# Turning softmax weights on TensorE: 128 queries at a time, or pairs of 64 on the two halves of the array's rows

## The chip, the cores and the metric

The kernel runs on one core of one Trainium2 chip. The metric is device time in microseconds. The other seven cores are idle.

## What is computed

The reference is a two-layer trunk over 256 latent tokens with 256 context tokens as a prefix, model width 1024. Each layer has a token-mixing part (a convolution branch, attention with 8 heads of 64, and gates) and a gated MLP with a short convolution. All is fp32. The part that the change touches is the attention:

```python
s_win = jnp.einsum("bhqd,bhiqjd->bhqij", q_r, k_win, preferred_element_type=jnp.float32) * scale
...
s_ctx = jnp.einsum("bhqd,bhcd->bhqc", q_r, k_ctx, preferred_element_type=jnp.float32) * scale
s = jnp.concatenate([s_win.reshape(b, h, GRID_W, n_win), s_ctx], axis=-1)
p = jax.nn.softmax(s, axis=-1).astype(v.dtype)
...
return (jnp.einsum("bhqij,bhiqjd->bhqd", p_win, v_win)
        + jnp.einsum("bhqc,bhcd->bhqd", p_ctx, v_ctx))
```

Latent queries see a window of latent keys (a bias that masks all other latent keys stands in for the window here) and all 256 context keys, so 512 keys in all. Context queries see the 256 context keys; they are computed in the first layer alone.

## The kernel before

Activations lie with channels on the partitions and tokens along the free dimension. A weight comes as a unit of 128 x 1024 in fp32 by a load on SP's queue (L155), is split into a high and a low part, `whi` by ScalarE (L158) and `wlo` by VectorE (L159), and each product is then three matmuls (L177, L178, L179). The buffers `raw`, `whi` and `wlo` rotate through four places each, so a load is issued only when the split of an earlier unit has freed its place. Loads of other weights (`in_wada`, L145) use the same places of `raw`, and the load of `sb` (`across`, L243, with a Silu in L245) stands behind them in SP's queue.

Side work is threaded between the matmul groups: each group calls `slot()`, which advances a list of generators by one step. Two of these matter here. `conv_run` and `layer_norm` put the 31 taps of the depthwise convolution on VectorE (L576, one instruction for a tap), and `Attention.step` does a step of the attention. The framework then orders the instructions of each engine ahead of time by its own estimates of their durations; `issue_after` adds constraints to that order. On the chip each engine takes its instructions in that order.

The attention goes by pairs of heads j (0 to 3); a pair's two heads lie on partitions 0 to 63 and 64 to 127. A step does three things in this order:

- `turn`: the softmax weights of the last step are turned, so that keys come onto the partitions.
- `values`: the weights that were turned in the step before are multiplied with V (L502), and the result is split into `oh` and `ol` (L508, L509).
- `products`: the scores of the next work item (L430). Two heads go at a time, on rows 0 to 63 and 64 to 127 of the array, into two banks. The softmax follows on VectorE (L448: bias and maximum; L453) and on ScalarE (L451: exponential; L454: scaling). For context queries these are L462, L467, L469 and L472.

A work item has four score tiles `pp` of 128 queries x 512: for latent queries two blocks of 128 queries by two heads; for context queries two heads by two pairs, each with two blocks of 128 queries by 256 keys side by side. Layer 0 has four latent items and two of context queries, layer 1 four latent ones, so `turn` runs ten times.

In `turn` each 128 x 128 block of `pp` is transposed by TensorE (L484, L489), with the block as the stationary operand and the identity as the moving one. Four blocks of one head fill one PSUM bank, and ScalarE copies the bank to `pT` (L485, L490). The banks are two of tag `sc`, then one of tag `pt` and one of the four of tag `main`; `products` then uses the same four tags. `values` reads `pT` as the moving operand, 256 queries wide.

Of the kernel before, what the change touches and what calls it, by code (L numbers as in the profile page):

```python
# [8 lines left out]
F32 = mybir.dt.float32  # L9
# [6 lines left out]
P = 128  # L16
# [3 lines left out]
S = 256  # L20
# [12 lines left out]
LAT, CTX = slice(0, S), slice(S, 2 * S)  # L33
# [12 lines left out]
def trunk(ctx: ExitStack, tc: tile.TileContext, xt, cvec, crow, wall, wada, params, bias_t, rope_t, out):  # L46
    nc = tc.nc
    pe, act, dve, pool, sp = nc.tensor, nc.scalar, nc.vector, nc.gpsimd, nc.sync
# [11 lines left out]
    def nm(s):  # L60
        uid[0] += 1
        return f"{s}_{uid[0]}"
# [3 lines left out]
    def psum(tag="main"):  # L66
        return psp.tile([P, 512], F32, tag=tag, bufs=BANKS[tag], name=nm(tag))

    def tmp(w=512):
        return tp.tile([P, w], F32, tag="t", bufs=5, name=nm("t"))  # L70
# [4 lines left out]
    def sl(w, i):  # L75
        return w[:, i * P : (i + 1) * P]
# [29 lines left out]
    start = ExitStack()  # L106
# [5 lines left out]
    ident = cp.tile([P, P], F32, name="ident")  # L112
# [260 lines left out]
    HALF = [slice(0, HD), slice(HD, P)]  # L373

    class Attention:
# [99 lines left out]

        def turn(self, what, its, pps):

            pts = [self.eb.tile([P, 4, S], F32, tag="pT", bufs=4, name=nm("pT")) for _ in range(2)]
            for n, tags in enumerate((("sc", "sc"), ("pt", "main"))):
                for i, pp in enumerate(pps[n]):  # L480
                    pt = psum(tags[i])
                    if what == LAT:
                        for kt in range(4):
                            pe.transpose(sl(pt, kt), sl(pp, kt), ident)  # L484
                        act.copy(pts[i][:, :, n * P : (n + 1) * P], pt.rearrange("p (k q) -> p k q", k=4))  # L485
                    else:
                        for t in range(2):
                            for kt in range(2):
                                pe.transpose(pt[:, kt * S + t * P : kt * S + (t + 1) * P], sl(pp, 2 * t + kt), ident)  # L489
                        act.copy(pts[i][:, 2 * n : 2 * n + 2, :], pt.rearrange("p (k q) -> p k q", k=2))  # L490
            js = [its[0][0]] if what == LAT else [it[0] for it in its]
            self.pv.append((what, js, pts))

        def values(self, what, js, pts, bank):
            po = psum(bank)
            kts = range(4) if what == LAT else range(2, 4)
            for n, j in enumerate(js):
                c = slice(n * S, (n + 1) * S)
                for kt in kts:
                    for i in range(2):  # L500
                        h = 2 * j + i
                        pe.matmul(  # L502
                            po[i * HD : (i + 1) * HD, c], self.V[kt][:, h * HD : (h + 1) * HD],
                            pts[i][:, 2 * n + kt - kts[0], :], start=kt == kts[0], stop=kt == kts[-1],
                        )
            for n, j in enumerate(js):
                c = slice(n * S, (n + 1) * S)
                act.copy(self.oh[j][:, what], po[:, c])  # L508
                dve.tensor_tensor(self.ol[j][:, what], po[:, c], self.oh[j][:, what].bitcast(F32), ALU.subtract)  # L509
# [11 lines left out]
    for k in range(KD):  # L521
        sp.dma_start(x[k], xt[k])
        q = tmp()
# [19 lines left out]
    for l in range(DEPTH):  # L543
# [5 lines left out]
        with ExitStack() if last else start as e1a:  # L549
# [68 lines left out]
            with ExitStack() as e1b:  # L618
# [98 lines left out]
                else:  # L717
                    sp.dma_start(rope, rope_t)
                    pg0 = [psum("sc") for _ in range(2)]
                    for uu in range(2):  # L720
                        wg = wunit(l, U_GLU0 + uu)
                        for i in range(2):
                            for kk in range(4):
                                k = 4 * uu + kk
# [59 lines left out]
                n = 0  # L784
# [16 lines left out]
            with ExitStack() as e1c:  # L801
# [71 lines left out]
                for n, pc in branch(U_CO, sh_, sl_):  # L873
                    t = tmp()[:, :T]
# [60 lines left out]
        with ExitStack() as e2:  # L935
# [115 lines left out]
            for streams, ns in [((0, 1), range(NB)), *(((s,), range(NB, KD)) for s in range(NS))]:  # L1051
                wu = None
                c = slice(streams[0] * S, (streams[-1] + 1) * S)
                for n in ns:
                    ps = psum()
                    for k in range(KF):
                        t = n * KF + k
# [19 lines left out]
            if last:  # L1077
                std, rs = small([P, 2], "red"), small([P, 2], "rs")
                pt = psum("pt")
# [133 lines left out]
```

## Time and profile before

| | |
|---|---|
| Median of 3 runs | 1129.97 us (1129.38 to 1132.16) |
| Span of the profiled execution, first to last instruction | 1127.4 us; what lies around it is not told apart, and the median is 2.6 us above the span |
| Granted TensorE clock | 0.998 |
| TensorE matmuls / weight loads, busy | 1115.5 us (99%) / 965.1 us (86%) |
| VectorE busy | 906.5 us (80%) |
| ScalarE busy | 565.7 us (50%) |
| Transposes in `turn` | 160: 128 in L484, 32 in L489 |
| Copies to `pT` | 40: 32 in L485, 8 in L490 |
| Conv taps L576 | 240, 140.6 us busy |

Times in views of the profile are microseconds from the start of the span. PE is TensorE's matmuls, PEld its weight loads, DVE is VectorE, ACT is ScalarE, SPq is SP's queue. Lines such as L484 are lines of the kernel. A view of the timeline gives start, duration, engine, line, operation, what is written from what, the shape (rows x columns of the stationary operand, then partitions x elements), and how many instructions are merged into the row; a bracket shows idle time and what ended it. The chain of waits gives start, duration and what the end of the program waited for at that time. The view of waits gives who waited for whom, microseconds in total, times, longest.

### The profile page before, as it was taken

What the parts mean: (1) busy time and instruction counts of PE and PEld (TensorE: products, weight loads), DVE (VectorE), ACT (ScalarE), POOL (GpSimd) and SP (SyncE); (2) the same over time, 40 slices, a digit from 0 to 9 for tenths busy, and PEclk for the clock granted to TensorE, in tenths of its full rate; (3) what the DMA queues carried; (4) which work ended last, traced back from release to release, by engine and by line L of the source; (5) the groups of instructions that cost most, each with busy time, mean ns of one, the idle gap of its engine ahead of it and who ended that gap; (6) DMA issues with size and microseconds to landing.
All of it is one profiled execution on the core that took longest, in us unless ns stands there. A gap on an engine that the chain in (4) does not pass through costs nothing.

```text
span 1127.4 us, 17780 instructions
## 1 busy us (share of the span) xinstructions
PE 1115.5 (99%) x6854; PEld 965.1 (86%) x6854; DVE 906.5 (80%) x1625; ACT 565.7 (50%) x937; POOL 17.2 (2%) x24
## 2 busy tenths in 40 slices
PE   9999999999999999999999999999999999999997
PEld 7678777787789988888888888989898999999997
DVE  4689999786778788888898555789996898988773
ACT  4347657542334543444334223544677667766642
POOL 0000000000000000000000000010000000000000
PEclk9999999999999999999999999999999999999999
DMA  8832231635734354545556656555533575665781
GB/s 325 310 100 89 92 117 38 200 99 198 248 120 145 110 170 133 184 152 155 165 181 205 214 188 197 176 194 174 154 109 120 180 247 175 187 193 182 213 274 57
DMA packets 53941, 190.83 MB, mean 169 GB/s; under 512 B 6240, under 2 KB 6496, under 8 KB 53856
## 3 DMA queue, kind: packets, MB, share of 16 engines
q1 hardware_dynamic: 53568, 189.65, 52.6%
q8 instruction: 54, 0.88, 0.3%
q14 instruction: 31, 0.25, 0.1%
q10 hardware_dynamic: 288, 0.04, 0.0%
HBM read 188.62 MB, written 1.05 MB: 168 GB/s over the span
## 4 chain that ended last, share of the span: by engine, by line
PE 85%; DVE 10%; DMA 2%; ACT 2%; issue 1%; POOL 0%; SPq 0%; DVEq 0%; ACTq 0%; POOLq 0%
PE main L177 25%; PE main L179 24%; PE main L178 24%; DVE cb L576 4%; PE main L629 4%; DVE wlo L159 2%; DMA raw<-in_wall 1%; PE sc L127 1%; PE sc L177 1%; PE sc L179 1%; PE sc L178 1%; PE po L200 1%; PE po L502 1%; DMA sb<-in_crow 1%; PE sc L430 0%
## 5 line engine op out<-in xcount | busy, mean ns | idle before, releaser
L177 PE MATMUL main<-h,whi 128*128 128x256 f32 (+1 forms) x1328 | 446.8, 337 | 0.0
L179 PE MATMUL main<-h,wlo 128*128 128x256 f32 (+1 forms) x1328 | 443.4, 335 | 0.5 <-DVE wlo L159 0.5
L178 PE MATMUL main<-h,whi 128*128 128x256 f32 (+1 forms) x1328 | 442.4, 333 | 0.0
L158 ACT CAST whi<-raw 128x1024 fp32r<-128x1024 f32 (+1 forms) x244 | 252.5, 1039 | 284.7 <-PE main L178 128.6
L159 DVE TENSOR_TENSOR wlo<-raw,whi 128x1024 fp32r<-128x1024 f32 (+1 forms) x244 | 293.7, 1209 | 113.3 <-ACT whi L158 108.6
L177 PEld LDWEIGHTS main<-h,whi 128*128 128x128 f32 x1328 | 249.5, 188 | 32.0 <-issue 3.9
L179 PEld LDWEIGHTS main<-h,wlo 128*128 128x128 f32 x1328 | 249.5, 188 | 28.9 <-DVE wlo L159 0.7
L178 PEld LDWEIGHTS main<-h,whi 128*128 128x128 f32 x1328 | 249.9, 188 | 28.1 <-issue 0.2
L576 DVE SCALAR_TENSOR_TENSOR cb<-u,par,cb 128x512 f32<-128x512 f32 (+1 forms) x240 | 140.6, 620 | 1.2
L261 DVE CUSTOM_DVE_ANT_0 t<-raw,sb,par 128x1024 bf16<-128x1024 f32 x100 | 126.9, 1280 | 1.4 <-ACT sb L245 1.2
L177 PE MATMUL main<-fh,whi 128*128 128x256 f32 (+1 forms) x386 | 123.0, 319 | 0.0
L178 PE MATMUL main<-fl,whi 128*128 128x256 f32 (+1 forms) x386 | 122.9, 319 | 0.0
L179 PE MATMUL main<-fh,wlo 128*128 128x256 f32 (+1 forms) x386 | 122.9, 318 | 0.0
L178 PEld LDWEIGHTS main<-fl,whi 128*128 128x128 f32 x386 | 72.7, 188 | 5.6
L177 PEld LDWEIGHTS main<-fh,whi 128*128 128x128 f32 x386 | 72.7, 188 | 5.6
L179 PEld LDWEIGHTS main<-fh,wlo 128*128 128x128 f32 x386 | 72.7, 188 | 5.5
L948 ACT ACTIVATE t<-main,par 128x512 f32<-128x512 f32 (+1 forms) x82 | 50.7, 669 | 35.3 <-PE main L179 35.3
L949 DVE SCALAR_TENSOR_TENSOR t<-main,par,t 128x510 f32<-128x510 f32 (+1 forms) x82 | 47.6, 616 | 8.2 <-ACT t L948 7.6
L952 DVE SCALAR_TENSOR_TENSOR t<-main,par,t 128x510 f32<-128x510 f32 (+1 forms) x82 | 46.6, 611 | 0.0
L356 ACT ACTIVATE h<-t,mod 128x256 fp32r<-128x256 f32 x56 | 25.2, 502 | 37.5 <-DVE t L355 37.4
L883 DVE SCALAR_TENSOR_TENSOR x<-main,mod,x 128x256 f32<-128x256 f32 x48 | 22.1, 480 | 23.6 <-PE main L179 23.4
L629 PE MATMUL main<-whi,h 128*128 128x512 f32 x128 | 40.6, 402 | 0.0
(217 smaller groups left out, 1198.0 us busy)
## 6 DMA issues: line engine op xcount, KB each, us to landing
raw<-in_wall SPq DMA_DIRECT2D x239, 512.0 KB, 4.2
raw<-in_wada SPq DMA_DIRECT2D x88, 512.0 KB, 4.4
bias<-in_bias_t SPq DMA_DIRECT2D x8, 640.0 KB, 4.4
row<-in_wada SPq DMA_DIRECT2D x8, 512.0 KB, 4.8
sb<-in_crow SPq DMA_DIRECT2D x5, 512.0 KB, 6.1
x<-in_xt SPq DMA_DIRECT2D x8, 256.0 KB, 4.6
raw<-in_wall SPq DMA_DIRECT2D x8, 256.0 KB, 6.8
out<-t SPq DMA_DIRECT2D x3, 256.0 KB, 2.1
```

What stands on the lines that cost most here:

```text
L158: act.copy(hi[:, c], r[:, c])
L159: dve.tensor_tensor(lo[:, c], r[:, c], hi[:, c].bitcast(F32), ALU.subtract)
L177: pe.matmul(ps, w[0], xh, start=start, stop=False)
L178: pe.matmul(ps, w[0], xl, start=False, stop=False)
L179: pe.matmul(ps, w[1], xh, start=False, stop=stop)
L261: dve.tensor_tensor_reduce(tmp().bitcast(BF16), r, v, 1.0, pr(l, BADA + n, 1), ALU.mult, ALU.add, mods[l][:, n, s : s + 1])
L356: high = act.activation(hi[:, c], y[:, c], AF.Identity, bias=b)
L576: dve.scalar_tensor_tensor(cb[j], src, w, cb[j], ALU.mult, ALU.add)
L629: pe.matmul(pv[t], h1[n == 1][k][:, c], w[n == 2][:, b], start=k + n == 0, stop=k == KD - 1 and n == 2)
L948: act.activation(c, pv_, AF.Identity, bias=pr(l, FDB + t, 1), scale=w[1])
L949: dve.scalar_tensor_tensor(c[:, :, 1:], pv_[:, :, : S - 1], w[0], c[:, :, 1:], ALU.mult, ALU.add)
L952: dve.scalar_tensor_tensor(c[:, :, : S - 1], pv_[:, :, 1:], w[2], c[:, :, : S - 1], ALU.mult, ALU.add)
```

## The change

A block of 128 queries is transposed as two matmuls of 64 queries, one on rows 0 to 63 of the array and one on rows 64 to 127. The first writes 64 columns of one bank and the second 64 columns of another. So the two banks of a pair of score tiles fill together: a bank now holds one half of the queries of both tiles, where it held all queries of one. ScalarE copies a bank with runs of 64 elements where it had 128, as many elements and as many copies as before. `pT` is one tile for both heads in place of two, with the same bytes and the same layout for `values`, which is otherwise unchanged. For context queries the four blocks of a tile are taken in the order that puts them into the same places as before. In the changed file, lines after `turn` have a number one higher.

```diff
         def turn(self, what, its, pps):
 
-            pts = [self.eb.tile([P, 4, S], F32, tag="pT", bufs=4, name=nm("pT")) for _ in range(2)]
+            pT = self.eb.tile([P, 2, 4, S], F32, tag="pT", bufs=2, name=nm("pT"))
             for n, tags in enumerate((("sc", "sc"), ("pt", "main"))):
+                outs = [psum(t).rearrange("p (i s q) -> p i s q", i=2, s=4) for t in tags]
                 for i, pp in enumerate(pps[n]):
-                    pt = psum(tags[i])
+                    for s in range(4):
+                        src = s if what == LAT else s % 2 * 2 + s // 2
+                        for pt, r in zip(outs, HALF):
+                            pe.transpose(pt[:, i, s], sl(pp, src)[r], ident[r, r])
+                for pt, r in zip(outs, HALF):
                     if what == LAT:
-                        for kt in range(4):
-                            pe.transpose(sl(pt, kt), sl(pp, kt), ident)
-                        act.copy(pts[i][:, :, n * P : (n + 1) * P], pt.rearrange("p (k q) -> p k q", k=4))
+                        act.copy(pT[:, :, :, n * P + r.start : n * P + r.stop], pt)
                     else:
-                        for t in range(2):
-                            for kt in range(2):
-                                pe.transpose(pt[:, kt * S + t * P : kt * S + (t + 1) * P], sl(pp, 2 * t + kt), ident)
-                        act.copy(pts[i][:, 2 * n : 2 * n + 2, :], pt.rearrange("p (k q) -> p k q", k=2))
+                        to = pT[:, :, 2 * n : 2 * n + 2].rearrange("p i k (t q) -> p i (k t) q", t=2)
+                        act.copy(to[:, :, :, r], pt)
             js = [its[0][0]] if what == LAT else [it[0] for it in its]
-            self.pv.append((what, js, pts))
+            self.pv.append((what, js, pT))
 
-        def values(self, what, js, pts, bank):
+        def values(self, what, js, pT, bank):
...
                         pe.matmul(
                             po[i * HD : (i + 1) * HD, c], self.V[kt][:, h * HD : (h + 1) * HD],
-                            pts[i][:, 2 * n + kt - kts[0], :], start=kt == kts[0], stop=kt == kts[-1],
+                            pT[:, i, 2 * n + kt - kts[0]], start=kt == kts[0], stop=kt == kts[-1],
                         )
```

## The prediction

> **What bounds the kernel now.** I read the page first, for the busy shares and the chain that ended last.
>
> ```profile
> PE   1115.5 (99%) x6854; PEld 965.1 (86%) x6854; DVE 906.5 (80%) x1625; ACT 565.7 (50%) x937; POOL 17.2 (2%) x24
> ...
> PE 85%; DVE 10%; DMA 2%; ACT 2%; issue 1%; POOL 0%; SPq 0%; DVEq 0%; ACTq 0%; POOLq 0%
> ```
>
> TensorE is busy nearly always, but a tenth of the chain is VectorE's. So the question is which engine ends last in the two stretches with attention (about 84 to 205 us, and 800 to 872). Busy time by stretch comes next: span, then PE, PEld, DVE, ACT.
>
> ```profile
> 160.00:180.00 20.00, 20.00 (x114) 15.80 (x113) 20.00 (x40) 13.95 (x26) 0.00 (x0) 1.00 0.33 102
> ...
> 820.00:840.00 20.00, 20.00 (x147) 17.35 (x146) 19.91 (x58) 15.29 (x34) 0.04 (x1) 1.00 0.41 129
> ```
>
> Both engines are full there, and the conv taps (L576) are what fills VectorE. What decides is the place where one of the two has to wait. The chain of waits, in order of time, shows it for layer 0:
>
> ```profile
> core 0 of [0], span 1127.4 us
> ...
> 198.98 0.75 DVE cb L576
> ...
> 200.73 1.15 DVE wlo L159
> ...
> 202.27 6.08 DMA sb<-in_crow
> ...
> 212.03 0.44 PE pt L224 x2
> ```
>
> VectorE's queue reaches a weight split (L159), which frees a buffer; only then does SP's queue issue the load of sb, ScalarE puts that through Silu, evicts the modulation products behind it in its queue, and TensorE may do the transposes of L224. TensorE gets there first. The view of waits:
>
> ```profile
> PE pt L224 <- ACT t L217: 1.1, 1, 1.1
> ```
>
> So up to 212.0 us layer 0 ends by VectorE's queue, and TensorE has 1.1 us to spare.
>
> **The transposes themselves.** Ten turns (eight for latents, two for context), each with 16 transposes. One turn in the chain, and the instructions of the line (min/median/max ns):
>
> ```profile
> 827.98 0.87 PE sc L484 x8
> 828.85 0.44 PE pt L484 x4
> 829.29 0.44 PE main L484 x4
> 829.73 1.88 PE po L502 x16
> ```
>
> ```profile
> L484 PEld LDWEIGHTS sc<-ident,pp x64: 138/141/144, 102.5 to 859.1; 128*128 128x128 f32 x64
> L484 PE MATMUL sc<-ident,pp x64: 270/272/275, 102.7 to 859.2; 128*128 128x128 f32 x64
> ```
>
> A turn takes 0.87 + 0.44 + 0.44 = 1.75 us, 109 ns for each transpose. The change makes it 32 transposes of 64 rows with 64 moving columns, alternating between the halves of the rows. The built program shows just that: 320 of 128x64 in place of 160 of 128x128, and nothing else moved on TensorE. Two things can set the new step. By the moving columns, half of 109 is 55 ns. By the weight load it depends on how long a transposing load holds the loader, because each half still loads 128 columns of pp. The nearest rows are plain loads:
>
> ```profile
> 12.80 1.86 PEld L517 LDWEIGHTS pt<-one,t 128*128 128x128 f32 x16 [0.41 <-issue]
> ```
>
> ```profile
> L502 PEld LDWEIGHTS po<-pT,V x144: 132/137/137, 113.8 to 869.4; 128*64 128x64 f32 x144
> ```
>
> L517 moves one column, so its pace is the loader's: sixteen loads in 1.86 us, less the length of one (0.19, as in the loads of L430 below), over 15, is 111 ns for 128 plain columns. The transposing load, at 141 ns, lasts as long as the plain load of 64 columns, 137; its hold is then about half of 111, some 57 ns. Bounds: 55 and 111 ns for a load; I take 57, by L502. Whether the halves work at once is shown by the products of 64 rows:
>
> ```profile
> 116.65 0.28 PE L430 MATMUL pt<-qk,qk 64*128 64x256 f32 x1
> 116.76 0.28 PE L430 MATMUL main<-qk,qk 64*128 64x256 f32 x1
> 116.77 0.28 PE L430 MATMUL pt<-qk,qk 64*128 64x256 f32 x1
> 116.88 0.28 PE L430 MATMUL main<-qk,qk 64*128 64x256 f32 x1
> ```
>
> ```profile
> 116.53 0.19 PEld L430 LDWEIGHTS sc<-qk,qk 64*128 64x128 f32 x1
> 116.53 0.19 PEld L430 LDWEIGHTS pt<-qk,qk 64*128 64x128 f32 x1
> ```
>
> Each half goes on every 120 ns, so two matmuls pass in 120, and two loads start at the same time. Hence 16 pairs x 57 = 0.91 us in place of 1.75.
>
> The Trainium skill (TensorE: Matmul & The Clock Gate, LDWEIGHTS (loading the stationary operand)) speaks against the change: a load's time goes with its columns, and 32 rows take as long as 128. L517 and L502 agree for plain loads (111 ns of pace for 128 columns). For transposing loads no row shows the pace; if it held there too, the pair would take what one transpose takes now.
>
> Going between whole-array and half-array work costs something as well:
>
> ```profile
> 829.66 1.49 PEld L502 LDWEIGHTS po<-pT,V 128*64 128x64 f32 x16 [0.17 <-issue]
> 831.53 0.53 PEld L430 LDWEIGHTS sc<-qk,qk 64*128 64x128 f32 x6 [0.39 <-issue]
> ```
>
> Some 0.2 us for one switch (0.39 holds the pace of an L502 pair, 0.2). The skill says the same (TensorEngine Tiling (Array Packing), Key Properties: a change of tiling mode drains the array). The change adds one switch ahead of the transposes. In the first turn of a layer, where products follow directly, one goes away again.
>
> Net on TensorE: 0.91 + 0.2 - 1.75 = -0.64 us for a turn that values follow.
>
> In the first turn of each layer that is worth nothing, because the products that follow wait for ScalarE's four copies, one after another:
>
> ```profile
> 105.04 0.61 ACT L485 COPY pT<-main 128x512 f32<-128x512 f32 x1
> ```
>
> ```profile
> 105.53 0.39 PE L430 MATMUL main<-qk,qk 64*128 64x512 f32 x1
> ```
>
> A copy of sc must now wait for both banks, 8 pairs (0.46 us) and the switch in place of 4 transposes (0.44): the copies start 0.2 us later there. The copies move as many elements in runs of 64 instead of 128; I cost that at nothing, and at most 0.1 us each.
>
> **What the saved time is worth.** Eight turns (five in layer 0, three in layer 1) x 0.64 = 5.1 us is the most. In layer 0 (four latent and two context turns) TensorE only arrives earlier at L224, where it waits for VectorE's queue: worth 0. Moreover the scheduler has put VectorE's instructions in another order. Of those that stand ahead of the split at 200.73 there is one more in the changed program, a conv tap: 0.75 us by the row at 198.98, somewhat less where its successor doesn't depend on it. VectorE has no idle time to take it up. Taken: +0.7.
>
> In layer 1 TensorE runs without a wait, but VectorE and ScalarE are close behind. The last softmax, and what it leads to:
>
> ```profile
> 852.29 0.48 DVE L576 SCALAR_TENSOR_TENSOR cb<-u,par,cb 128x256 f32<-128x256 f32 x1
> 852.69 0.69 DVE L448 CUSTOM_DVE_ANT_1 sc<-sc,bias 128x512 f32<-128x512 f32 x1
> ```
>
> ```profile
> 867.05 2.99 ACT L158 CAST whi<-raw 128x1024 fp32r<-128x1024 f32 x3
> ```
>
> ```profile
> 868.18 3.50 DVE L159 TENSOR_TENSOR wlo<-raw,whi 128x1024 fp32r<-128x1024 f32 x3 [0.52 <-ACT whi L158]
> ```
>
> ```profile
> 870.29 0.28 PE L179 MATMUL main<-h,wlo 128*128 128x256 f32 x1
> ```
>
> L448 waits for nothing but its turn behind the taps. ScalarE then runs exponentials, scalings, sigmoids and copies back to back up to the casts at 867.05; the first of the three splits ends about 868.18 + 1.2 = 869.4, and TensorE wants it at 870.29. That leaves 0.9 us. In the changed program two more taps stand ahead of that L448, 2 x 0.4 to 0.5 = about 1.0 us. So the split comes 0.1 us after TensorE's old time, and whatever TensorE saved in three turns (1.9 us) is lost in this wait. Bounds: if ScalarE has slack that I don't see, the 0.9 + 1.0 turns into a gain of up to 1.2; if the taps cost 0.6 each, the loss is 0.3. Taken: +0.2.
>
> Sum: +0.7 + 0.2 = +0.9 us on a span of 1127.4. The median of the runs, 1129.97, lies 2.6 above that span, and I carry that over: 1130.9. A difference under 0.3% (3.4 us) is about what a measurement of this kernel can't tell from none.
>
> **The rivals.**
>
> *The weight load sets the pace* (the page's rule above, taken for transposing loads): 16 pairs x 111 = 1.78, with the switch 1.98, +0.23 a turn. In layer 0, 6 x 0.23 = 1.4 stays under the room at L224 (1.1 + 0.7); in layer 1 the first copies start 0.6 later and three turns add 0.7, about 1.3 in place of my 0.2. Total +2.0: 1132.0; with 120 ns a pair, as L430 goes, +3. For: each half loads 128 columns. Against: the 141 ns.
>
> *The halves don't run at once and every transpose keeps its 109 ns*, because it isn't its columns that set it: 32 x 109 + 0.2 = 3.69, +1.94 a turn. Ten turns 19.4, less the 1.1 of room at L224: +18, 1148. It decides from 116 ns a pair on (1.8 us of room in six turns of layer 0); halfway, at 170 ns, six turns cost 6.9 - 1.1 and four 4.6, so +10. For: no row has two transposes at once, and 64 instructions in 0.91 us are denser than any stretch of the trace. Against: L430's rows.
>
> *VectorE doesn't hold and TensorE's time gets through*: -5.1, 1124.9. The load of sb would have to be issued that much earlier; the full VectorE speaks against it.
>
> **How the numbers follow.** My case 0.57, alone 1129.3 to 1132.3; load-bound 0.20, a quarter of it over 0.3%; one at a time 0.15, between 1134 and 1148; getting through 0.08. Within 0.3%: 0.57 + 0.15 = 0.72. Slower: 0.15 + 0.05 = 0.20. Faster: 0.08. The range takes in the first two cases and the mild half of the third: 1128.7 to 1137.
>
> **What would show it.** Right: transposes of a half 55 to 60 ns apart and two at once, a turn of about 0.9 us; the wait at L224 grown from 1.1 to some 5 us (five turns x 0.64, and the later tap); the load of sb issued 0.7 us later in its stage; TensorE waiting for a split near 870 us. Wrong: pairs 110 ns or more apart (second case), single transposes 109 apart (third), L224 without a wait or earlier than 212 us (fourth), or a total more than 3 us off.

## The result, and the profile after

The changed kernel takes 1135.25 us in the median of its first 5 runs (1131.49 to 1139.76), against 1129.97 for the kernel before: a ratio of 1.0042, 95% interval 1.0024 to 1.0061. In a later comparison, beside 23 runs of the kernel before, it was 1135.64 against 1131.89, ratio 1.0049 (1.0030 to 1.0068). So it is slower: both intervals lie above 1. The ratios are above 0.3%, which the prediction took for the least that can be told from none, but the intervals reach down to 0.24 and 0.30%. The profiled execution has a span of 1133.5 us, 6.1 more than before.

The page of the changed kernel, busy shares and shares of the chain:

```profile
PE 1117.4 (99%) x7014; PEld 962.3 (85%) x7014; DVE 906.8 (80%) x1625; ACT 564.6 (50%) x937; POOL 17.2 (2%) x24
...
PE 81%; DVE 12%; ACT 3%; issue 2%; DMA 1%; POOL 0%; DVEq 0%; ACTq 0%; SPq 0%; POOLq 0%
```

The totals hardly tell anything: 160 more matmuls, 1.9 us more of TensorE. The transposes themselves did what was meant. The end of a turn in layer 1, in the timeline of the changed kernel:

```profile
849.87 0.71 PE L485 MATMUL sc<-ident,pp 64*128 64x64 f32 x16
850.42 0.22 PE L485 MATMUL pt<-ident,pp 64*128 64x64 f32 x1
850.42 0.22 PE L485 MATMUL main<-ident,pp 64*128 64x64 f32 x1
850.48 0.22 PE L485 MATMUL pt<-ident,pp 64*128 64x64 f32 x1
850.48 0.22 PE L485 MATMUL main<-ident,pp 64*128 64x64 f32 x1
...
851.01 0.65 PE L503 MATMUL po<-pT,V 128*64 128x256 f32 x4
```

Two halves start at the same time, and pairs follow every 60 to 63 ns. From the first transpose to the first of the values it is 1.14 us.

To see where the time goes I compare the start of one and the same gate or weight product (L177 to L179; same number in TensorE's order) in two traces. The table gives, for each kernel that ran, how much later than in the first profile of the kernel before it starts, in us, at seven places named by that profile's time. 22.6 us lies ahead of every instruction that any of these kernels moves, 184.4 behind the latent turns of layer 0, 212.5 behind L224, 737.8 at the end of layer 0, 870.2 at the end of attention in layer 1, 925 ahead of a normalization in layer 1, and 1118 at the end. Where the text says, as the prediction does, that layer 0 ends early or late, it means the end of its attention, at 212.5 us.

| Kernel | 22.6 | 184.4 | 212.5 | 737.8 | 870.2 | 925 | 1118 |
|---|---|---|---|---|---|---|---|
| changed, first profile | 3.07 | 1.80 | 3.96 | 4.66 | 5.34 | 5.37 | 6.01 |
| changed again (e1) | -0.55 | -1.79 | 0.29 | 1.20 | 1.87 | 1.96 | 4.78 |
| latents alone (e2) | -0.49 | -1.14 | -1.45 | -1.46 | -0.86 | -0.81 | -0.19 |
| context alone (e3) | 0.63 | 0.03 | 0.21 | 0.25 | 0.19 | 0.25 | 3.45 |
| held taps (e4) | 0.62 | -0.50 | 5.04 | 5.94 | 6.89 | 6.84 | 9.97 |
| before, L217 first (e5) | -0.14 | -0.20 | -1.54 | -1.88 | -1.91 | -1.93 | -1.51 |
| changed, L217 first (e6) | 0.00 | -1.26 | 0.69 | 1.09 | 1.78 | 1.74 | 5.74 |
| and values first (e7) | 3.27 | 2.02 | 3.38 | 3.86 | 5.06 | 5.12 | 6.42 |
| and softmax first (e8) | 0.04 | -1.19 | 1.67 | 2.27 | 0.49 | 0.49 | 5.00 |
| changed, square first (e9) | 3.29 | 2.02 | 4.39 | 4.86 | 5.47 | 5.43 | 6.53 |
| before, square first (e10) | 0.36 | 0.33 | 0.07 | -0.28 | -0.25 | -0.27 | 0.65 |
| halves, eased (e11) | -0.17 | -0.75 | -1.05 | -1.01 | -2.78 | -2.78 | -1.56 |
| whole, eased (e12) | 0.01 | -0.01 | -1.35 | -1.37 | -1.43 | -1.44 | -0.77 |

Half of the 6.01 us of the first profile were there before the change could act. Stretches of the changed kernel's start (span, then busy time and count of PE, PEld, DVE, ACT, POOL, then granted clock, DMA share, GB/s):

```profile
12.00:16.00 4.00, 4.00 (x37) 3.17 (x36) 0.16 (x1) 0.00 (x0) 0.12 (x1) 0.77 1.04 419
16.00:20.00 4.00, 4.00 (x24) 3.47 (x17) 1.37 (x5) 1.30 (x3) 0.90 (x1) 0.50 1.03 396
```

The granted clock was 0.50 for 6.8 us there, where the profile of before has 1.00:

```profile
16.00:20.00 4.00, 4.00 (x26) 3.21 (x25) 3.36 (x9) 2.80 (x7) 0.06 (x1) 1.00 1.01 394
```

A second half clock stands in the last context turn of layer 0, as TensorE's timeline and two stretches show:

```profile
194.39 0.71 PE L485 MATMUL sc<-ident,pp 64*128 64x64 f32 x16
196.25 0.27 PE L485 MATMUL pt<-ident,pp 64*128 64x64 f32 x1 [1.14 <-ACT pp L472]
...
196.64 0.27 PE L485 MATMUL pt<-ident,pp 64*128 64x64 f32 x1
...
197.04 0.27 PE L485 MATMUL pt<-ident,pp 64*128 64x64 f32 x1
...
197.76 1.28 PE L503 MATMUL po<-pT,V 128*64 128x256 f32 x8
```

```profile
195.10:198.50 3.40, 2.02 (x25) 1.32 (x26) 3.33 (x7) 3.38 (x10) 0.00 (x0) 1.00 0.00 0
198.50:201.90 3.40, 3.40 (x15) 1.92 (x12) 3.22 (x6) 3.39 (x7) 0.00 (x0) 0.50 0.00 0
```

TensorE comes early, and then waits for one scaling (L472) after another. The stretch with 2.02 us of work in 3.40 is followed by one at half the clock. The same turn in the kernel before has no wait:

```profile
193.40:196.80 3.40, 3.40 (x29) 2.33 (x28) 3.22 (x6) 3.37 (x7) 0.00 (x0) 1.00 0.02 5
```

In layer 1 the values of the last item now wait. Timeline rows of the changed kernel:

```profile
858.45 0.69 DVE L448 CUSTOM_DVE_ANT_1 sc<-sc,bias 128x512 f32<-128x512 f32 x1
...
872.51 0.39 ACT L509 CAST oh<-po 128x256 fp32r<-128x256 f32 x1
872.93 0.42 DVE L510 TENSOR_TENSOR ol<-po,oh 128x256 fp32r<-128x256 f32 x1 [6.01 <-ACT oh L509]
873.41 1.30 PE L503 MATMUL po<-pT,V 128*64 128x256 f32 x10 [0.69 <-DVE ol L510]
```

In the kernel before they follow without a wait, 0.42 us behind the end of `ol`:

```profile
867.23 0.42 DVE L509 TENSOR_TENSOR ol<-po,oh 128x256 fp32r<-128x256 f32 x1 [6.01 <-ACT oh L508]
...
868.07 1.95 PE L502 MATMUL po<-pT,V 128*64 128x256 f32 x16
```

So the first reading was: a start that has nothing to do with the change (if it is chance), two places that the change made late, and a clock that reacts to the waits. The experiments take these apart.

### The profile page after: what moved, and what is told of

Its sections match the earlier page's. It is cut to its first block, busy times and chain, and to the rows that moved or that the text cites. A ratio compares the mean times of both kernels' runs of the same rounds, so it can differ in the third digit from the quotient of the medians.

```text
span 1133.5 us, 18094 instructions
## 1 busy us (share of the span) xinstructions
PE 1117.4 (99%) x7014; PEld 962.3 (85%) x7014; DVE 906.8 (80%) x1625; ACT 564.6 (50%) x937; POOL 17.2 (2%) x24
## 3 DMA queue, kind: packets, MB, share of 16 engines
HBM read 188.62 MB, written 1.05 MB: 167 GB/s over the span
## 4 chain that ended last, share of the span: by engine, by line
PE 81%; DVE 12%; ACT 3%; issue 2%; DMA 1%; POOL 0%; DVEq 0%; ACTq 0%; SPq 0%; POOLq 0%
PE main L177 23%; PE main L179 23%; PE main L178 23%; DVE cb L577 5%; PE main L630 4%; DVE wlo L159 3%; DMA raw<-in_wall 1%; PE sc L127 1%; PE sc L177 1%; PE sc L179 1%; PE sc L178 1%; PE po L200 1%; ACT whi L158 1%; ACT pp L467 1%; ACT pp L472 1%
## 5 line engine op out<-in xcount | busy, mean ns | idle before, releaser
L177 PE MATMUL main<-h,whi 128*128 128x256 f32 (+1 forms) x1328 | 447.2, 337 | 0.0
L179 PE MATMUL main<-h,wlo 128*128 128x256 f32 (+1 forms) x1328 | 443.5, 335 | 0.4 <-DVE wlo L159 0.4
L177 PEld LDWEIGHTS main<-h,whi 128*128 128x128 f32 x1328 | 249.6, 188 | 32.4 <-issue 4.7
L179 PEld LDWEIGHTS main<-h,wlo 128*128 128x128 f32 x1328 | 249.7, 188 | 29.0 <-DVE wlo L159 0.7
L177 PE MATMUL main<-fh,whi 128*128 128x256 f32 (+1 forms) x386 | 123.0, 319 | 0.0
L179 PE MATMUL main<-fh,wlo 128*128 128x256 f32 (+1 forms) x386 | 122.9, 318 | 0.0
L177 PEld LDWEIGHTS main<-fh,whi 128*128 128x128 f32 x386 | 72.7, 188 | 5.6
L179 PEld LDWEIGHTS main<-fh,wlo 128*128 128x128 f32 x386 | 72.7, 188 | 5.6
```

Of the source, the lines that this page charges most:

```text
L177: pe.matmul(ps, w[0], xh, start=start, stop=False)
L179: pe.matmul(ps, w[1], xh, start=False, stop=stop)
```

## The experiments

**e1: the changed kernel again.** No edit.

> The changed kernel once more, unedited. Its first profile lost 3.1 us before 22 us, where TensorE's granted clock was 0.50 for 6.8 us, ahead of every instruction that the change touches; from there to the end it lost another 3.0. Theory A (the early half clock falls at random, the loss behind it belongs to the change): runs fall into two groups, near 1132.2 (1133.5 - 3.1 + 1.8) without the early half clock and near 1135.3 with it; a profile without it starts layer 0 level with the kernel before and ends 2 to 3 us behind. Rival B (the early half clock belongs to the changed program): every run at 1135 or more, and every profile with 0.50 ahead of 22 us.

Median 1135.64 us (1134.22 to 1141.59); the profile has 1.00 throughout the start and starts 0.55 us ahead. So rival B falls: the early half clock doesn't come with the change each time, and it comes without it too. In the 14 profiles of this study it comes in six (6.8 us long in three, 3.4 in three), e3 among them, and e10, which is the kernel before but for an order near 934 us. But the long form was seen in three of the seven profiles with halves in all turns and in none of the seven others. Nothing that the change moves lies ahead of it, yet so few profiles don't exclude that it is more frequent there. A stretch of e10:

```profile
16.00:20.00 4.00, 4.00 (x21) 3.75 (x20) 3.55 (x7) 2.94 (x6) 0.00 (x0) 0.70 1.02 397
```

But theory A was wrong in its times: without the early half clock this execution still took 1134.22 us, since something came that the first profile had not. In the context turn TensorE lost 1.6 us without a half clock (the stretch with 2.15 us of work stayed at 1.00), and L224 ended layer 0 by the load of sb. Stretch, waits, and chain of e1:

```profile
190.00:193.40 3.40, 2.15 (x28) 1.36 (x26) 3.32 (x7) 3.40 (x13) 0.00 (x0) 1.00 0.00 0
```

```profile
PE pt L224 <- ACT t L217: 1.6, 1, 1.6
```

```profile
201.47 1.15 DVE wlo L159
...
203.01 5.63 DMA sb<-in_crow
...
210.00 2.00 ACT sb L245 x2
...
212.32 0.44 PE pt L224 x2
```

From the start to 212.5 us e1 loses 0.84, as the first profile lost 0.89 with a half clock and no wait at L224: two causes of like size, of which the later one counts. Then, behind 925 us, where nothing was changed, e1 loses 2.8:

```profile
PE pt L326 <- DVE ss L312: 1.8, 1, 1.8
```

```profile
928.49 4.70 DMA raw<-in_wall
...
934.25 0.41 ACT t L308
```

```profile
934.10:937.50 3.40, 1.58 (x14) 1.38 (x13) 2.81 (x6) 3.16 (x7) 0.00 (x0) 1.00 0.79 288
937.50:940.90 3.40, 3.40 (x18) 3.40 (x18) 2.49 (x4) 1.98 (x3) 0.70 (x1) 0.51 0.96 306
```

A cast that waits for a weight load stands in ScalarE's queue ahead of a square on whose sum TensorE waits (0.5 us in the profile before, by the row below); and a half clock follows the wait.

```profile
PE pt L326 <- DVE ss L312: 0.5, 1, 0.5
```

**e2: halves in the latent turns alone.**

```diff
+                if what == LAT:
...
+                else:
+                    for i, (pp, t) in enumerate(zip(pps[n], tags)):
+                        pt = psum(t)
...
+                            for t in range(2):
+                                for kt in range(2):
+                                    pe.transpose(pt[:, kt * S + t * P : kt * S + (t + 1) * P], sl(pp, 2 * t + kt), ident)
```

> Halves for the eight latent turns alone; the two context turns are transposed by 128 queries as before. VectorE's order is that of the changed kernel, later taps and all. Theory A (in layer 0 the changed kernel loses in its last context turn: TensorE waits 1.1 us for scalings, and a half clock follows there): no wait and no half clock in that turn, L224 waits again for the load of sb that comes 0.7 us late; layer 0 ends 0.7 to 0.9 behind, layer 1 adds 1.4 by its later softmax: span 1129.7, time 1131.5, plus 3.1 if the early half clock falls. Rival C (the context softmax is late by VectorE's order, whatever the turn): TensorE waits in the context turn here too, the half clock comes all the same, and the time is that of the changed kernel, 1132.2.

Median 1132.23 us beside 1131.89 (ratio 1.0008, 0.9994 to 1.0023). No half clock, as theory A says; but the context softmax is 1.3 us late here too, by VectorE's order, and TensorE loses 1.0 us in that turn, so rival C is half right. And layer 0 ended 0.96 early, not 0.7 late. ScalarE's timeline shows why:

```profile
205.09 0.37 ACT L217 COPY t<-sc 128x256 f32<-128x256 f32 x1
208.70 1.28 ACT L245 ACT_TABLE_LOAD   x1 [3.24 <-DMA sb<-in_crow]
209.99 2.01 ACT L245 ACTIVATE sb<-sb 128x1024 f32<-128x1024 f32 x2
```

The framework happened to put L217 ahead of the Silus, so the load of sb (as late as in e1) stops nobody. Layer 1 loses 0.60 as the changed kernel does.

**e3: halves in the context turns alone.** The condition of e2 is turned round (`what == CTX`); VectorE's softmaxes then have as many taps ahead of them as in the kernel before.

> Halves for the two context turns alone; latent turns as before. VectorE's order is exactly that of the kernel before. Theory A: with the softmax in its old place TensorE reaches the last context turn no earlier than before, so it waits at most 0.3 us there, no half clock; two turns save 1.2 us, which ends in the wait at L224; layer 1 is as before: span 1127.4, time 1129.2 to 1130.0. Rival D (transposes by halves make the half clock by themselves, being short and sparse): the clock falls to 0.5 near 198 us, and L224 comes 1 to 2 us late: 1130.5 to 1132.

Median 1132.80 us (ratio 1.0017, 1.0002 to 1.0033). No wait and no half clock in the context turns: rival D falls, transposes by halves don't bring the half clock by being short. Layer 0 ends 0.42 ahead of its start, layer 1 loses nothing. The 3.2 us at the end are the wait at 934 us with its half clock.

**e4: the taps held back.**

```diff
             def conv_tap(j, t):
+                m = min(AT[tap_at.n], len(tap_at.mx))
+                tap_at.n += 1
+                if m:
+                    with tc.issue_after(tap_at.mx[m - 1].ins):
+                        return conv_do(j, t)
+                return conv_do(j, t)
```

`AT` holds, for each tap, how many softmax instructions of VectorE stood ahead of it in the kernel before.

> The changed kernel with each conv tap kept behind the softmax behind which it stood before (an ordering constraint alone; no work added), so every L448 and L462 has as many taps ahead of it as in the kernel before, and the split ahead of the load of sb has one less than before. Theory A (the later taps are what the change costs): no wait in the context turns beyond 0.5 us, no half clock there, sb at its old time or 0.4 us earlier, and in layer 1 the three turns save up to 1.9 us of which 0.9 to 1.9 gets through: span 1126 to 1127.4, time 1128 to 1129.5. Rival E (the halves cost by something other than VectorE's order): at least 2 us behind the kernel before, as the changed kernel is without its early half clock.

Median 1140.36 us (ratio 1.0084, 1.0067 to 1.0102), the slowest of all: theory A's repair fails. In layer 1 the last L448 has the old number of taps ahead of it and is still 1.3 us late against 737.8. The reason is in the distance from a tap to its successor. Set beside the order of the built program, every tap whose successor is a tap of the same buffer `cb` takes some 0.12 us longer: 0.52 us in place of 0.40 in layer 1, 0.79 in place of 0.66 in layer 0. Ahead of the first L462 of the last context item the kernel before has 5 such pairs and e4 22; in layer 1, ahead of the last L448, 11 and 18. By that estimate they cost 2.0 and 0.8 us. That L462, which has its old 97 taps ahead of it, is 1.9 us late. In layer 0 TensorE waits 4.0 us for scalings, and the clock halves for two stretches:

```profile
PE pt L491 <- ACT pp L478: 4.0, 2, 2.9
```

```profile
192.90:196.30 3.40, 0.67 (x8) 0.40 (x8) 3.33 (x7) 3.38 (x10) 0.00 (x0) 1.00 0.53 154
196.30:199.70 3.40, 2.03 (x14) 1.35 (x16) 3.22 (x6) 3.39 (x8) 0.00 (x0) 0.50 0.00 0
```

**e5: the kernel before with L217 ahead of the Silus.**

```diff
-        with tc.issue_after(lastev[0].ins):
-            act.activation(t, t, AF.Silu)
...
-                        yield from ada_all([(0, 8)])
+                        ev = ada_rows(ada_products(0, 8, "sc"))
+                        silu_of(sb0)
+                        yield
+                        yield
+                        ada_sums(0, 8, ev)
```

> The kernel before, with ScalarE's copy of the modulation products (L217) put ahead of the two Silus that wait for the load of sb; nothing else moved. Theory F (layer 0 of the kernel before ends by VectorE's queue through the load of sb, and by nothing else): the wait of 1.1 us at L224 goes, the next groups follow 1.1 us earlier than in the kernel before at the same start, and the median falls by about 1.1 us. Rival G (another wait stands right behind it): less than 0.3 us.

Median 1128.92 us beside 1131.18 (ratio 0.9984, 0.9973 to 0.9994): faster than the kernel before. Layer 0 ends 1.34 us earlier, counted from 184.4: theory F.

**e6: the same order in the changed kernel.** The edit of e5.

> The changed kernel with that same order of ScalarE (L217 ahead of the Silus). In the changed kernel layer 0 ended 0.84 and 0.88 us later than in the kernel before, counted from the same start. Theory F: L224 has no wait; what is left is the wait for the scalings in the last context turn, and layer 0 ends 0.4 us late without a half clock in that turn, about 2 late with one. Rival H (the context turn sets layer 0's end by itself, sb is hidden): still 0.8 or more late without a half clock.

Median 1135.07 us (ratio 1.0037, 1.0022 to 1.0052). L224 waits no more, but this profile has the half clock in the context turn, and layer 0 ends 0.69 late (2 expected with one). The context turn takes what L224 gives.

**e7: and values ahead of the turn** where no products follow.

```diff
...
+            for f in (turns, vals) if self.todo else (vals, turns):
+                f()
```

> As the run before, and in the steps that have no further products the values stand ahead of the turn, so TensorE has 1.95 us of work while ScalarE scales the last softmax. Theory A (the context turn loses by waiting, not by its transposes): no wait for L472, no half clock near 195 to 203 us, TensorE's savings in layer 0 get through: layer 0 ends 1.2 to 1.8 us earlier than in the kernel before, counted from the same start; layer 1 still loses 0.7. Median 2 us below the changed kernel's, more where that had the half clock. Rival D (the transposes by halves bring the half clock by being short): the half clock stays, no gain.

Median 1134.81 us (ratio 1.0034, 1.0022 to 1.0047). The wait for L472 goes, and no half clock comes there; but the turned weights must now be copied with nothing between, and values wait for that:

```profile
PE sc L514 <- ACT pT L502: 2.8, 1, 2.8
...
PE po L514 <- ACT pT L499: 1.8, 1, 1.8
```

Layer 0 ends 0.11 late, layer 1 loses 1.2. A wait has moved, no more. These waits are longer than the one for L472 was, and no half clock follows them here. In e8, which has the first of them too, one does.

**e8: and softmaxes ahead of the taps, in layer 1** (with the edit of e7).

```diff
-                        if taps:
-                            conv_tap(*taps.pop(0))
+                        if taps and last and att.mx is not None:
+                            with tc.issue_after(att.mx.ins):
+                                conv_tap(*taps.pop(0))
```

> As the run before, and in layer 1 each conv tap is kept behind the softmaxes that were there when it was listed, so the last L448 has 210 taps of both layers ahead of it in place of 238. Theory J (layer 1 loses since VectorE is full and the last softmax stands behind its taps): the last softmax comes some 10 us earlier, no wait for po (L510) or a split near 870, and TensorE's savings of layer 1 get through: from 737 to 880 us the kernel gains 1.0 to 1.5 on the kernel before in place of losing 0.7; median 2 us below the run before. Rival K (the taps that are put off delay the normalization after attention): the gain is given back between 880 and 905 us.

Median 1133.28 us (ratio 1.0016, 1.0001 to 1.0031). Theory J holds: from 737.8 to 870.2 the kernel gains 1.78 where the changed one lost 0.68, with no wait for `po`. Rival K is wrong about the place (nothing is lost up to 925), but 4.5 us go behind it, in the wait at 934 us. Chain of e8:

```profile
928.43 6.98 DMA raw<-in_wall
```

**e9 and e10: the square ahead of later casts**, in the changed kernel and in the kernel before.

```diff
+            hold[0] = sss[0].sq if last else None
...
-            act.copy(hi[:, c], r[:, c])
+            if hold[0] is None:
+                act.copy(hi[:, c], r[:, c])
+            else:
+                with tc.issue_after(hold[0].ins):
+                    act.copy(hi[:, c], r[:, c])
```

> The changed kernel; in layer 1 ScalarE's casts of the up-projection's fifth and later weight units are put behind the last square (L308) of the output projection, on whose sum TensorE waits near 934 us (L326). Until now such a cast, which waits for its load, stood ahead of that square. Theory L (the wait at 934 us goes with the duration of one weight load, in both kernels; where it passes some 2 us the clock halves behind it): the wait at L326 falls under 0.6 us, no half clock near 940, from 880 to 942 us at most 0.5 is lost against the first profile of the kernel before, where the changed kernels lost 0.6 to 5; median from 1135 to 1132 or 1133. Rival M (the weights come too late for TensorE anyway): the wait moves to a split behind 934 us, and the time stays.

> The same reordering in the kernel before. Theory L: its slower half of runs (1131 to 1135) thins out, median 1129.2 to 1130.2 against 1131.2 to 1131.9; what then lies between this and the run before is the change's own cost, 2 to 3 us: 0.85 in layer 0, 0.7 in layer 1, and half clocks in the context turn. Rival M: the median stays.

The half clock near 940 us came in five of the ten profiles without this order, and in none of the four with it (e9 to e12). The wait at L326 is gone, but 0.9 to 1.1 us come back a step later, so rival M has part of the truth:

```profile
PE po L347 <- POOL rs L342: 0.9, 1, 0.9
```

e10 has a median of 1129.88 us beside 1131.09 (ratio 0.9987, 0.9976 to 0.9999), e9 1134.86 (1.0033, 1.0018 to 1.0047). So the changed kernel's loss does not lie at 934 us: with that place calm in both, it is still 5.0 us between the medians. The two profiles differ by 6.0 us of span, of which 2.9 ahead of 22.6 us, by early half clocks of 6.8 and 3.4 us; the other 3.1 split into 1.4 up to 212.5 (e10 gains 0.3, e9 loses 1.1 with a half clock), 0.8 up to 737.8, 0.6 up to 870.2 and 0.3 behind.

**e11 and e12: halves and whole blocks with the three orders.** e11: latent turns by halves, context turns whole, with the edits shown under e5, e8 and e9 (not that of e7). e12: the kernel before with the same three edits.

> Halves in the latent turns alone (whole blocks in the context turns), with three reorderings: L217 ahead of the Silus in layer 0, softmaxes ahead of the later taps in layer 1, the square ahead of the later casts. Theory N (once no other engine stands behind TensorE, the shorter turns are worth their time): layer 0 ends about 1.0 earlier than in the kernel before, layer 1's attention gains 1.0 to 1.8 more, nothing of it goes at 934: median 1127 to 1128, and below the next run by 0.5 to 1.5 us. Rival O (the time saved meets the next wait each time): level with the next run or above it.

> The kernel before (blocks of 128 queries in all turns) with the same three reorderings. Layer 0 ends 1.3 us earlier as it did with the first of them alone; layer 1 has at most 0.5 us of waits to lose. Theory N: median 1128 to 1129, 0.5 to 1.5 above the run before. Rival O: level with it or below.

e11 has a median of 1127.31 us beside 1131.09, ratio 0.9966 (0.9955 to 0.9978): it beats both kernels. e12 has 1129.52, ratio 0.9986 (0.9971 to 1.0000). In layer 1 e11 gains 1.77 us, in layer 0 it ends 0.88 ahead of its start where e12 ends 1.36 ahead. All waits of TensorE from 785 to 880 us in e11:

```profile
PE sc L441 <- ACT pT L500: 0.2, 1, 0.2
```

So the shorter turns are worth 1.8 us in layer 1 once VectorE and ScalarE don't stand behind them, and less than nothing in layer 0, where VectorE's order is as in the changed kernel. All ten turns by halves with these three orders, or with an order of VectorE that suits layer 0, were not run.

## Why the prediction was right or wrong

The time lies in the range (1128.7 to 1137.0), but the forecast was 4.35 us too low and the outcome is the one that had 0.20: slower by over 0.3%. That it lies in the range is luck: my case alone ended at 1132.3, and the rest was there for rivals that fell. By its own last sentence (a total more than 3 us off) it was wrong. Point by point:

- **The turn.** Right on TensorE. 62 ns for a pair in place of 57, two at once; the third, fourth and fifth turn of layer 0 (one for context, two for latents) and the third of layer 1 gained 0.59 to 0.62 us each against 0.64 forecast. Both rivals that priced the transposes higher fell. The Trainium skill's rule for loads (TensorE: Matmul & The Clock Gate, LDWEIGHTS (loading the stationary operand)), by which 128 columns cost as much for 64 rows, does not give the pace here: two such transposing loads pass in 62 ns.
- **The products behind a turn.** The prediction let products wait for ScalarE's copies in the first turn of a layer alone. In layer 0 that is as forecast: there is a wait of 0.25 us, and TensorE's distance to the kernel before is the same ahead of that turn and behind it (-0.57 us in e1). But the second turn, which values follow, loses 0.56: one more tap stands ahead of its item's L448, so ScalarE comes 0.67 us late to the softmax and then to the copies, and the products behind the values wait for these. VectorE's rows, of the kernel before and of e1, and TensorE's waits in e1:

```profile
102.60 3.39 DVE L576 SCALAR_TENSOR_TENSOR cb<-u,par,cb 128x512 f32<-128x512 f32 x5
```

```profile
102.04 4.06 DVE L577 SCALAR_TENSOR_TENSOR cb<-u,par,cb 128x512 f32<-128x512 f32 x6
```

```profile
PE sc L430 <- ACT pT L488: 1.1, 2, 0.8
```

In the first turn of layer 1, 0.55 are lost: in ScalarE's queue an eviction that waits for VectorE stands between the copies, where it stood behind them in the kernel before.

```profile
816.36 0.38 ACT L754 ACTIVATE qk<-main 128x256 fp32r<-128x256 f32 x1 [0.36 <-DVE t L749]
```

With softmaxes first (e8, e11) that turn loses 0.07. So it is the order of the other engines that costs, and not the wait for both banks that the prediction had in mind.
- **Layer 0 ends by VectorE's queue and sb.** Right in kind, and the change's savings there were worth nothing; +0.84 measured in e1 against +0.7 is partly luck. Counted from the same place the load of sb is issued 1.3 us later, not 0.7 (203.01, and 0.55 of earlier start, against 202.27), since besides the one more tap (0.66 us) another one took 1.20 us in place of 0.74, at 151.44 us, while a GpSimd instruction ran; but the load then takes 5.63 us in place of 6.08. e2, e5 and e11 show the cause: with L217 ahead of the Silus layer 0 ends 0.9 to 1.4 us early. But the room at L224 grew to 1.6 us, not 5. I had priced the turns as if TensorE were free to come early. In the last context turn it met a softmax that VectorE's new order had made 1.3 us later, and lost 1.6 us there. I had read that order only for the split ahead of sb and for layer 1.
- **Layer 1.** The step was right and its slack was not. The last softmax came 1.10 us late (1.0 forecast): 858.45, less 4.66 of shift, against 852.69. I gave it 0.9 us of room at the split. But the values come first: in the kernel before `ol` (L509) was done at 867.65 and L502 began at 868.07, 0.42 us of room. 1.10 less 0.42 is 0.68, which is what the stretch lost (0.2 forecast). e8 and e11 show that it was VectorE's queue: with softmaxes first the loss of 0.68 turns into a gain of 1.8. The loss in the first turn and the gain in the third don't show in the sum, since this last wait sets the end.
- **The end of layer 0, 212.5 to 737.8 us.** No step of the prediction spoke of it. The seven kernels with halves in all ten turns lose 0.4 to 0.9 us there, in a wait for a sum (L326); the others lose nothing. It has the form of the wait at 934 us: a cast that waits for a weight load stands ahead of the square. That load is issued at the same place in all 14 profiles, counted from 212.5 us (within 0.1 us), and takes 4.0 to 4.5 us in these seven and 3.3 to 3.7 in the others. In the chains of the kernel before and of the changed one:

```profile
730.64 3.66 DMA raw<-in_wall
```

```profile
734.62 4.34 DMA raw<-in_wall
```

The instructions of this stretch come in the same order in the changed kernel as in the kernel before. Why the load takes longer is open.
- **What was carried from the span to the median.** I added 2.6 us to the quietest sort of execution; every run whose span is on record took 1.7 to 1.9 us more than its span, so some 0.8 of the 2.6 was the distance from that execution to the median. The kernel before ran from 1128.8 to 1135.1 us in later comparisons, with medians of 1131.1 to 1131.9. The changed kernel's profiles have half clocks in the context turn (five of seven with halves in all turns, none of seven others). That is the part of the loss that no sum of waits holds: the last context turn cost 1.6 us in e1 and, with a half clock behind the wait, 3.3 in e6.

The sum of what was shown, in e1's terms: 0.84 up to 212.5, 0.91 up to 737.8, 0.67 up to 870.2, 2.4 us in place of the 0.9 forecast; the rest between the medians, 1.3 us (e1) to 2.9 us (first runs), fits the half clocks. Which of them came in a timed run wasn't seen, but the span and the mean granted clock of each run are on record, and the time at half clock is 2 x (1 - clock) x span. It is an average of 13.4 us in the 11 runs of the changed kernel and 10.1 in 85 of the kernel before; 11.9 in e9 and 7.7 in e10. Among the runs of one kernel, a microsecond more at half clock goes with some 0.45 us more of time (a straight line through all runs, each taken against its kernel's mean). By that estimate the half clocks are 1.5 us of the 4.8 by which the means of changed kernel and kernel before differ, and 1.9 of the 4.7 between e9 and e10. What is left, 3.3 and 2.8 us, is near the waits that the profiles show (2.4 in e1 up to 870 us, and 3.1 between e9 and e10).

## What to carry to other kernels

A shorter step on the engine that is busy all the time pays only as far as the next consumer has room. Look for the first use of every buffer behind the late engine (here `po`, 0.42 us), not for the use that is easiest to name (the split, 0.9). And read the order that a scheduler makes at every softmax, since a change of 0.6 us on one engine moved VectorE's taps by one or two at most of the softmaxes. Where such a change loses, the engine order is worth a try before the change is dropped: with three changes of order (e11) the same transposes gave 1.8 us in layer 1, against 0.1 with whole blocks (e12).

## What the runs showed of the hardware

- A half clock lasted 3.41 us or twice that (apart from the one in which every profile ends), and its place against the program differs from run to run. What brings it isn't shown. Stretches of 3.4 us with 0.67, 1.58, 2.02 and 2.20 us of TensorE work were followed by a half clock; one with 2.15 (e1) and one with 1.60 (e7) were not, so busy time alone doesn't decide. The rows of e9 and e7:

```profile
195.50:198.90 3.40, 2.20 (x26) 1.44 (x27) 3.29 (x8) 3.38 (x9) 0.00 (x0) 1.00 0.00 0
```

```profile
871.30:874.70 3.40, 1.60 (x17) 1.06 (x16) 1.74 (x2) 3.40 (x6) 0.00 (x0) 1.00 0.30 113
```

The Trainium skill (TensorE: Matmul & The Clock Gate, HAM oscillation — how this bites in real kernels) names idle gaps over some 3.4 us as what to avoid. Here stretches with a longest gap of 1.1 (changed kernel) and 1.8 us (e1, at 934) were followed by a half clock; the stretch of e7, with a gap of 1.8, was not. The wait of 2.8 us lies within one stretch in e8, which leaves it 0.92 us of work, and is followed by a half clock; in e7 it is shared out between two, with 2.13 and 1.89 us of work, and is not.
- The same page of the Trainium skill (Part 4: PE-mode transpose) says that a transpose doesn't count as busy in the same way. The two rows above agree with that: 1.35 of the 2.20 us were transposes and the clock halved, none of the 1.60 were and it didn't. But they count for something: of the 2.15 us in e1, 1.35 were transposes too, and the clock stayed, where 1.58 us without any (e1, at 934) were followed by a half clock. The traces don't tell whether these transposes are of the kind that the page speaks of.
- At the start of the program six of 14 profiles have a half clock near 14 us. Those with 3.4 us of it start 0.4 to 0.6 us later than the first profile of the kernel before, those with 6.8 us 3.1 to 3.3: as much as half of the effect that was studied.
- From the start of a conv tap to the next instruction it is some 0.12 us longer if that is a tap of the same buffer: 0.52 against 0.40 us for 128x256, in all 12 such pairs of the kernel before and in none of its 57 others. An order that holds taps back paid for that (e4).
